# A written round for the attention loop: ordering edges on four engines, pairs and turned parts at fixed places

## The chip, the cores and the metric

The kernel runs on one core of one Trainium2 chip. The metric is device time in microseconds (us). Engines are named as the profile names them: PE (TensorE matmul), PEld (its weight load), DVE (VectorE), ACT (ScalarE), POOL (GpSimd) and SP (SyncE, which issues the DMAs). Each of them takes its instructions in the order of its own queue.

## The reference, cut to what matters

Two layers of a hybrid backbone over 1024 latent tokens and 256 context tokens, width 1024. In each layer one input projection feeds three mixers (attention, a bidirectional mLSTM, a pooling mixer); their outputs are joined, projected by `w_out`, added to the residual, normalised, and a SwiGLU follows. The change touches the attention and what is run beside it:

```python
def one_block(qi):                    # 128 query rows, 8 heads of 64, 2 key/value heads
    s = einsum('bqhgd,bkhd->bhgqk', qi, k) * d ** -0.5
    p = softmax(s, -1)
    return einsum('bhgqk,bkhd->bqhgd', p, v)
...
xl = xl + g1_l * (concatenate([att_l, ml_l, pool_l], -1) @ w_out)
```

Latent queries see 1280 keys (1024 latent, 256 context). In the first layer the context queries are computed too and see 256 keys.

## The kernel before, in words

Numbers are kept as pairs of f16 (a high part and the rest), so a product is three matmuls. The program is written with a tile library: it records instructions, and a scheduler of the library then chooses, engine by engine, the order in which they stand in the queues, by a cost model of its own and by the buffers that are free.

The attention loop of a layer works through *units*. A unit is one head and one tile of 128 query rows against 1280 keys; in the first layer there are 64 of these and 4 units of four heads against 256 keys, in the second layer 64. For a unit:

- `front` (L1303): six matmuls write the **scores** into `Sp`, three banks of PSUM with two buffers (L1311, PE). DVE takes the row maximum over 1280 columns (L1315, `mx<-Sp`) and scales it (L1320, `mx<-mx,rq`). ACT takes the **exponential** into `pf` (f32, two buffers) and adds up the rows into `sums`.
- `split` (L1330): the high part of `pf` is copied to `phl` in f16 (ACT, at L152; for one unit in eight DVE, L1339), POOL subtracts it to get the rest (`phl<-pf,phl`), and a transposing DMA on SP's queue turns `phl` into `pT` (L1345, five buffers). For ten units a layer, the *turned* ones, PE transposes `pf` in three *parts* of 4, 4 and 2 blocks into a bank `turn` (L1354), ACT copies each part to `pT` and DVE subtracts.
- `values` (L1361) takes two units, a *pair*. DVE takes the reciprocal of `sums` (L1366). PE spreads it over a bank `pv` (two matmuls, L1369, `pv<-idn,sums`) and ACT copies it out (`ao<-pv`). Then 60 matmuls (L1376) multiply `pT` by the values into another part of the same bank. DVE multiplies by the spread reciprocals (`ao<-pv,ao`), ACT copies the high part to `mixT` (`T<-ao`; mixT lies in the buffer `T1`, shown as T) and DVE subtracts for the rest (`T<-ao,T`).

One turn of the loop (L1453) writes the front of unit i, the split of unit i-1, one step of *fill*, and the values of units i-5 and i-4. A fill step (L1387) is twelve matmuls of the output projection into a bank `pwo` and one DVE addition into the residual (`X<-pwo,prm,X`). A new weight tile for it is split into its f16 parts by an ACT copy and a DVE subtraction (`hl<-st`, `hl<-st,hl`; both at helper lines L152 and L166). `budget` sets how often a step comes. Helper `bank` has two buffers, shared by `pv`, `turn`, `pwo` and the norms.

Of the kernel before, what the change touches and what calls it, by code (L numbers as in the profile page):

```python
# [9 lines left out]
F32 = mybir.dt.float32  # L10
# [8 lines left out]
P = 128  # L19
# [61 lines left out]
@with_exitstack  # L81
def hybrid_kernel(ctx: ExitStack, tc: tile.TileContext, I, out, dbg=None):
    nc = tc.nc
    V, S, G, TE, DMA = nc.vector, nc.scalar, nc.gpsimd, nc.tensor, nc.sync
    MUL, ADD, SUB, MAX, MIN = ALU.mult, ALU.add, ALU.subtract, ALU.max, ALU.min
    dbg = dbg or {}

# [33 lines left out]
    def bank3(name="S"):  # L121
        return cur["s"].tile([P, 1536], F32, tag="S", name=name)
# [10 lines left out]


    mm = TE.matmul
    order = mybir.DependencyInfo(mybir.DependencyClass.NoSync, mybir.DependencyReason.DATA)
    tabs = {"last": [], "pre": None, "kind": None}

    def after(i, j):
# [601 lines left out]
    for l in range(DEPTH):  # L741
# [555 lines left out]
        class Unit:  # L1297
# [4 lines left out]

            def front(self):  # L1303
                qt, nk, k0, n = self.qt, self.nk, self.k0, self.n
                Sp = bank3("Sp")
# [12 lines left out]
                h0 = self.hs[0]  # L1318
                if ne == 1:
                    tabs["mx"] = V.tensor_scalar(mx[:, :1], mx[:, :1], rq[:, 1, qt, h0:h0 + 1], LN4096, op0=MUL, op1=ADD).ins  # L1320
                else:
                    tt(mx[:, :ne], mx[:, :ne], rq[:, 1, qt, h0:h0 + ne], MUL)
                    tabs["mx"] = V.tensor_scalar(mx[:, :ne], mx[:, :ne], LN4096, None, op0=ADD).ins
                self.pf = pt_((P, NTOK), F32, "pf", PFB)
                for e, h in enumerate(self.hs):
                    act(self.pf[:, e * nk:(e + 1) * nk], Sp[:, e * nk:(e + 1) * nk], AF.Exp, bias=mx[:, e:e + 1],
                        scale=rq[:, 0, qt, h:h + 1],
                        accum_out=self.qs[1][:, h:h + 1])

            def split(self):  # L1330

                i, n, pf = self.i, self.n, self.pf
                if i in turned:
                    self.pT = pt_((P, 2, 10, P), F16, "pT", PTB)
                    self.parts = [self.turn(k, min(4, 10 - k)) for k in range(0, 10, 4)]
                    return
                hl = pt_((P, 2, NTOK), F16, "phl", PHB)
                if i % 8 == 0:
                    V.tensor_copy(hl[:, 0, :n], pf[:, :n])  # L1339
                else:  # L1340
                    act(hl[:, 0, :n], pf[:, :n])
                tt(hl[:, 1, :n], pf[:, :n], hl[:, 0, :n], SUB, G)
                self.pT = pt_((P, 2, 10, P), F16, "pT", PTB)
                if n == NTOK:
                    DMA.dma_start_transpose(out=self.pT.rearrange("p a k c -> p (a k) c"), in_=hl.rearrange("p a t -> p (a t)"))  # L1345
                else:
                    for a in range(2):
                        DMA.dma_start_transpose(out=self.pT[:, a, :n // P], in_=hl[:, a, :n])
# [11 lines left out]
        def values(us, pair):  # L1360

            qt, sums = us[0].qt, us[0].qs[1]
            nkt, k0 = us[0].nk // P, us[0].k0
            hs = (2 * pair, 2 * pair + 1)
            kv = pair // 2
            V.reciprocal(sums[:, hs[0]:hs[0] + 2], sums[:, hs[0]:hs[0] + 2])  # L1366
            pb = bank("pv")
            for g, h in enumerate(hs):
                mm(pb[64 * g:64 * g + 64, P:2 * P], sums[:, h:h + 1].to_broadcast([P, 64]), idn, start=True, stop=True)  # L1369
            u = f2k((P, 2, P), F32, "ao")  # L1370
            act(u[:, 0], pb[:, P:2 * P])
            for kt in range(nkt):
                for j, (a, b) in enumerate(TERMS):
                    for g, h in enumerate(hs):
                        un = us[g if len(us) == 2 else 0]
                        mm(pb[64 * g:64 * g + 64, 0:P], qkv[:, 6, b, k0 + kt * P:k0 + (kt + 1) * P][:, kv * 64:kv * 64 + 64],  # L1376
                           un.pT[:, a, un.hs.index(h) * nkt + kt], start=(kt == 0 and j == 0), stop=(kt == nkt - 1 and j == 2),
                           skip_group_check=True)
            tt(u[:, 1], pb[:, 0:P], u[:, 0], MUL)
            q = slice(qt * P, (qt + 1) * P)  # L1380
            act(mixT[:, pair, 0, q], u[:, 1])
            tt(mixT[:, pair, 1, q], u[:, 1], mixT[:, pair, 0, q], SUB)

        def wout(w, k0, m, t0, n, pb):
            for k in range(4):
# [48 lines left out]
        units = []  # L1434
# [7 lines left out]
        nt = {}  # L1442
        fill = fills()
        nu = len(units)
        turned = [u.i for u in units if len(u.hs) == 1][5::6]
        budget = 0.0
        fill_ffn = first_ffn()

# [1 line left out]

            return (1.1 if part < 0.9 else 2.5) if last else 0.8 if part < 0.2 else 1.5

        for i in range(nu + 5):  # L1453
            now[0] = i
            if i < nu:
                units[i].front()
            parts = []
            if 1 <= i <= nu:
                units[i - 1].split()
                parts = units[i - 1].parts  # L1460
            if parts:
                parts.pop(0)()
            if i >= 3:
                budget = min(budget + pace(i / nu), 3.0)
                if budget > 0:
                    c = next(fill, None)
                    if c is None:
                        c = next(fill_ffn, 0)
                    budget -= c
            if parts:  # L1470
                parts.pop(0)()
            if i >= 5:
                u = units[i - 5]
                if len(u.hs) > 1:
                    for e in range(0, len(u.hs), 2):
                        values([u], u.hs[e] // 2)
                elif u.hs[0] % 2 == 0:
                    values([u, units[i - 4]], u.hs[0] // 2)
                if u.hs[-1] in (6, 7) and u.qt < 8:
                    done[0] = u.qt  # L1480
                units[i - 5] = u = None
            while parts:
                parts.pop(0)()
            pump()
        for _ in fill:
            pass
        units = fill = None
# [544 lines left out]
```

## Time and profile before

| what | value |
|---|---|
| median of 3 runs | 2888.27 us (2887.95 to 2888.49) |
| profiled execution | 2884.12 us, its span 2882.4 us |
| PE busy over the span | 2631.7 us (91%) |
| DVE busy | 1951.8 us (68%) |
| ACT busy | 1412.3 us (49%) |
| POOL busy | 1234.7 us (43%) |
| DMA: the hardware queue | 38.4% of 16 engines |

A busy share is a mean over stages with different limits. The two attention loops lie at about 376 to 700 us and 1879 to 2170 us of the span; what bounds them is read from the timeline of those stretches, and not from the shares of the table.

### The profile page before, as it was taken

What the parts mean: (1) busy time and instruction counts of PE and PEld (TensorE: products, weight loads), DVE (VectorE), ACT (ScalarE), POOL (GpSimd) and SP (SyncE); (2) the same over time, 40 slices, a digit from 0 to 9 for tenths busy, and PEclk for the clock granted to TensorE, in tenths of its full rate; (3) what the DMA queues carried; (4) which work ended last, traced back from release to release, by engine and by line L of the source; (5) the groups of instructions that cost most, each with busy time, mean ns of one, the idle gap of its engine ahead of it and who ended that gap; (6) DMA issues with size and microseconds to landing.
All of it is one profiled execution on the core that took longest, in us unless ns stands there. A gap on an engine that the chain in (4) does not pass through costs nothing. (4 is left out here: it accounts for less than half of the span.)

```text
span 2882.4 us, 54835 instructions
## 1 busy us (share of the span) xinstructions
PE 2631.7 (91%) x21819; PEld 1521.2 (53%) x21819; DVE 1951.8 (68%) x3439; ACT 1412.3 (49%) x2816; POOL 1234.7 (43%) x959
## 2 busy tenths in 40 slices
PE   7999978887889999999999999878877799999997
PEld 4875555555545555555554674545545344444444
DVE  5458866678866565656665657877778766665666
ACT  5345556666534443434344445466666444444453
POOL 1123444455444443444443213444454554555551
PEclk9999999999999999999999999999999999999999
DMA  9534486677122222222212222487774111111211
GB/s 290 149 109 127 131 186 119 124 135 145 56 73 81 81 88 88 81 81 88 74 45 76 67 60 62 123 155 133 131 143 118 44 59 45 59 60 50 67 52 74
DMA packets 579797, 283.20 MB, mean 98 GB/s; under 512 B 311048, under 2 KB 568916, under 8 KB 579028
## 3 DMA queue, kind: packets, MB, share of 16 engines
q1 hardware_dynamic: 579364, 279.62, 38.4%
q8 instruction: 171, 2.80, 0.4%
q14 instruction: 86, 0.70, 0.1%
q10 hardware_dynamic: 176, 0.07, 0.0%
HBM read 176.19 MB, written 20.87 MB: 68 GB/s over the span
## 5 line engine op out<-in xcount | busy, mean ns | idle before, releaser
L1927 PEld LDWEIGHTS <-hlp 128*128 128x128 f16 x5040 | 492.2, 98 | 606.1 <-issue 30.5
L1927 PE MATMUL Swb<-T,hlp 128*128 128x512 f16 x1920 | 444.7, 381 | 28.7 <-DVE sg L166 13.5
L169 POOL TENSOR_TENSOR phl<-pf,phl 128x1280 f16<-128x1280 f32 (+1 forms) x112 | 292.4, 2613 | 313.7 <-ACT phl L152 209.7
L166 DVE SCALAR_TENSOR_TENSOR hlp<-ws,hlp 128x512 f16<-128x512 f32 (+1 forms) x320 | 228.4, 720 | 150.0 <-ACT hlp L152 121.8
L152 ACT ACTIVATE hlp<-ws 128x512 f16<-128x512 f32 (+1 forms) x320 | 163.6, 518 | 218.9 <-PE Swb L1927 87.6
L152 ACT ACTIVATE pf<-Sp,mx,rq 128x1280 f32<-128x1280 f32 (+1 forms) x144 | 189.9, 1320 | 129.1 <-DVE mx L1320 103.8
L1927 PE MATMUL Swc<-T,hlp 128*128 128x512 f16 x960 | 227.2, 379 | 0.0
L1927 PE MATMUL Swb<-tq,hlp 128*128 128x512 f16 x960 | 220.7, 379 | 2.3 <-ACT T L152 2.3
L1311 PE MATMUL Sp<-T 128*128 128x512 f16 (+1 forms) x800 | 182.0, 355 | 44.1 <-ACT pf L152 42.1
L1387 PE MATMUL pwo<-T,hl 128*128 128x512 f16 (+1 forms) x960 | 194.0, 350 | 30.9 <-DVE X L166 14.9
L466 PE MATMUL pfm<-T,hl 128*128 128x512 f16 (+1 forms) x1032 | 218.3, 365 | 2.6 <-ACT E L152 2.4
L1315 DVE TENSOR_REDUCE mx<-Sp 128x1 f32<-128x1280 f32 (+1 forms) x132 | 194.5, 1474 | 33.1 <-PE Sp L1311 32.5
L152 ACT ACTIVATE T<-sg 128x512 f16<-128x512 f32 (+1 forms) x170 | 100.2, 600 | 228.5 <-POOL sg L169 153.7
L166 DVE SCALAR_TENSOR_TENSOR hlp<-st,hlp 128x256 f16<-128x256 f32 (+1 forms) x201 | 141.8, 709 | 89.5 <-ACT hlp L152 74.7
L1939 PE MATMUL dx<-T,hlp 128*128 128x256 f16 x1440 | 177.9, 273 | 12.2 <-DVE hlp L166 6.4
L169 POOL TENSOR_TENSOR ws<-st 128x256 f32<-128x256 f32 (+1 forms) x97 | 102.1, 1061 | 180.4 <-DMA st<-in_w_ffn_down_dram 82.3
L169 POOL TENSOR_TENSOR X<-X,T 128x512 f32<-128x512 f32 x80 | 113.6, 1420 | 149.4 <-DVE X L166 112.2
L1927 PE MATMUL Swa<-T,hlp 128*128 128x512 f16 x720 | 169.1, 380 | 0.0
L1939 PEld LDWEIGHTS <-hlp 128*128 128x128 f16 x1440 | 139.3, 100 | 44.6 <-issue 10.8
L152 ACT ACTIVATE hlp<-st 128x256 f16<-128x256 f32 (+1 forms) x201 | 101.2, 510 | 112.8 <-PE Swb L1927 71.7
L466 PEld LDWEIGHTS <-hl 128*128 128x128 f16 x1032 | 100.8, 102 | 97.9 <-issue 21.6
L1387 PEld LDWEIGHTS <-hl 128*128 128x128 f16 x960 | 95.2, 101 | 108.4 <-issue 42.3
(327 smaller groups left out, 4969.1 us busy)
## 6 DMA issues: line engine op xcount, KB each, us to landing
T<-in_w_ada_dram SPq DMA_DIRECT2D x48, 512.0 KB
rawa<-in_w_ada_dram SPq DMA_DIRECT2D x48, 512.0 KB
st<-in_w_in_dram SPq DMA_DIRECT2D x32, 512.0 KB
st<-in_w_out_dram SPq DMA_DIRECT2D x64, 256.0 KB
st<-in_w_ffn_gate_dram SPq DMA_DIRECT2D x32, 512.0 KB
st<-in_w_ffn_up_dram SPq DMA_DIRECT2D x30, 512.0 KB
st<-in_w_ffn_down_dram SPq DMA_DIRECT2D x30, 512.0 KB
xs<-X SPq DMA_DIRECT2D x4, 2048.0 KB
```

The source lines that it names most:

```text
L152: b = S.activation(o, i, f, **kw).ins
L166: V.scalar_tensor_tensor(o, a, s, b, op0=o0, op1=o1)
L169: (e or V).tensor_tensor(o, a, b, op=op)
L466: mm(o, w[:, a, k, :], h[:, k, b, t0:t0 + n], start=(k == 0 and j == 0), stop=(k == nk - 1 and j == 2))
L1311: mm(Sp[:, e * nk + b0:e * nk + b0 + m], ql, qkv[:, 4 + h // 4, a, k0 + b0:k0 + b0 + m], start=(a == 0), stop=(a == 1), skip_group_check=True)
L1315: r = V.tensor_reduce(mx[:, :ne], Sp[:, :n].rearrange("p (e k) -> p e k", e=ne), axis=AX.X, op=MAX)
L1387: mm(pb, w[:, a, k, :], mixT[:, k0 + k, b, t0:t0 + n], start=(k == 0 and j == 0), stop=(k == 3 and j == 2))
L1927: mm(o, w[:, a, k, :], B[:, b], start=(s in "172" and k == 0 and j == 0), stop=(k == kh(i) - 1 and j == 2), skip_group_check=True)
L1939: mm(dbank[i][:, r * 256:(r + 1) * 256], w[:, a, k, :], B[:, b], start=(first and k == 0 and j == 0), stop=(not first and k == kh(i) - 1 a ...
```

## The change: what it does

Every call on DVE, ACT, POOL and PE inside the loop goes through a wrapper, and each instruction gets an ordering edge to the one before it on its engine. The scheduler can then no longer choose: each of the four queues holds the loop's instructions as they are written. DMAs have no such edges. The loop itself is written in another order, the values are split in two at a `yield`, and they are taken one turn later (units i-6 and i-5):

```diff
+            def call(*a, **k):
+                b = f(*a, **k)
+                if row["on"]:
+                    if self.key in row:
+                        tc.add_manual_dep(b.ins, row[self.key].name, order, reason="written order")
+                    row[self.key] = b.ins
+                return b
...
+    V, S, G, TE = (InRow(e, k) for k, e in enumerate((nc.vector, nc.scalar, nc.gpsimd, nc.tensor)))
...
-                if i % 8 == 0:
-                    V.tensor_copy(hl[:, 0, :n], pf[:, :n])
-                else:
-                    act(hl[:, 0, :n], pf[:, :n])
+                act(hl[:, 0, :n], pf[:, :n])
...
-            tt(u[:, 1], pb[:, 0:P], u[:, 0], MUL)
+            yield
+            o = pb[:, 2 * P:3 * P]
+            tt(o, pb[:, 0:P], u, MUL)
             q = slice(qt * P, (qt + 1) * P)
-            act(mixT[:, pair, 0, q], u[:, 1])
-            tt(mixT[:, pair, 1, q], u[:, 1], mixT[:, pair, 0, q], SUB)
+            act(mixT[:, pair, 0, q], o)
+            tt(mixT[:, pair, 1, q], o, mixT[:, pair, 0, q], SUB)
...
-        turned = [u.i for u in units if len(u.hs) == 1][5::6]
+        turned = [u.i for u in units if len(u.hs) == 1][4::6]
...
+        in_row(True)
+        parts = []
+        for i in range(nu + 6):
...
+            for g in vals:
+                next(g)
+            if 1 <= i <= nu:
+                units[i - 1].split()
+            for g in vals:
+                next(g, None)
+            if 1 <= i <= nu:
+                parts += units[i - 1].parts
+            if len(parts) > 2:
+                parts.pop(0)()
             if i < nu:
                 units[i].front()
...
             if parts:
                 parts.pop(0)()
+            if i < nu:
+                units[i].exps()
             if i >= 3:
-                budget = min(budget + pace(i / nu), 3.0)
-                if budget > 0:
+                budget = min(budget + pace(i / nu), 4.0)
+                while budget > (2.0 if vals and i < nu else 0):
```

`vals` is filled in every second turn, the *even* one of a pair of turns; the fill steps then fall into the *odd* turn, all but a few. The product `o` now lies in the PSUM bank `pv` and no longer in SBUF. A turned unit is always an even one now.

Three places show what stands in the queues. First, DVE in the second layer, around the additions of the output projection. Before:

```order
L166 SCALAR_TENSOR_TENSOR hl<-st,hl 128x512
L169 TENSOR_TENSOR ao<-pv,ao 128x128
L1315 TENSOR_REDUCE mx<-Sp 128x1
L169 TENSOR_TENSOR T_72<-ao,T_72 128x128
L1320 TENSOR_SCALAR mx<-mx,rq 128x1
L1315 TENSOR_REDUCE mx<-Sp 128x1
L1320 TENSOR_SCALAR mx<-mx,rq 128x1
L166 SCALAR_TENSOR_TENSOR X<-pwo,prm_142,X 128x512
L1315 TENSOR_REDUCE mx<-Sp 128x1
L1366 RECIPROCAL sums<-sums 128x2
```

DVE in the same layer now, from the maximum of an odd turn to that of the next even one (the wrapper's line, L96, stands for all):

```order
L96 TENSOR_REDUCE mx<-Sp 128x1
L96 TENSOR_SCALAR mx<-mx,rq 128x1
L96 SCALAR_TENSOR_TENSOR hl<-st,hl 128x512
L96 SCALAR_TENSOR_TENSOR X<-pwo,prm_142,X 128x512
L96 RECIPROCAL sums<-sums 128x2
L96 TENSOR_TENSOR pv<-pv,ao 128x128
L96 TENSOR_TENSOR T_72<-pv,T_72 128x128
L96 TENSOR_REDUCE mx<-Sp 128x1
```

The weight split and the addition into X now stand in front of the reciprocal in every pair that has them, and no maximum stands between them.

Second, ACT in the second layer's loop. Before:

```order
L152 ACTIVATE ao<-pv 128x128
L152 ACTIVATE pf,sums<-Sp,mx,rq 128x1280
L152 ACTIVATE phl<-pf 128x1280
L152 ACTIVATE T_72<-ao 128x128
L152 ACTIVATE pf,sums<-Sp,mx,rq 128x1280
L152 ACTIVATE ao<-pv 128x128
L152 ACTIVATE pf,sums<-Sp,mx,rq 128x1280
L152 ACTIVATE T_72<-ao 128x128
```

ACT in the second layer's loop now:

```order
L96 ACTIVATE pf,sums<-Sp,mx,rq 128x1280
L96 ACTIVATE phl<-pf 128x1280
L96 ACTIVATE pf,sums<-Sp,mx,rq 128x1280
L96 ACTIVATE hl<-st 128x512
L96 ACTIVATE ao<-pv 128x128
L96 ACTIVATE phl<-pf 128x1280
L96 ACTIVATE T_72<-pv 128x128
L96 ACTIVATE pf,sums<-Sp,mx,rq 128x1280
```

The copy `ao`, for which the value matmuls wait, stood between exponentials at changing distances; it now stands behind both exponentials of the pair in front.

Third, PE at a turned unit of the second layer, with buffer numbers. Before (`pf_23052` holds the exponentials of `Sp_23042`, the unit ahead of `Sp_23128`):

```order
L1311 MATMUL Sp_23128<-T2_73 128x512
L1311 LDWEIGHTS T2_73
L1311 MATMUL Sp_23128<-T2_73 128x256
L1354 MATMUL turn_23141<-idn_75,pf_23052 128x128 x4
L1387 LDWEIGHTS hl_22820
L1387 MATMUL pwo_23153<-T1_72,hl_22820 128x512
```

PE at a turned unit now (`pf_23397` holds the exponentials of `Sp_23387` itself):

```order
L96 MATMUL Sp_23387<-T2_73 128x512
L96 LDWEIGHTS T2_73
L96 MATMUL Sp_23387<-T2_73 128x256
L96 MATMUL turn_23400<-idn_75,pf_23397 128x128 x4
L96 LDWEIGHTS T2_73
L96 MATMUL Sp_23407<-T2_73 128x512
```

The first turned part stood behind the scores of the following unit; it now stands in front of them, right behind the scores of its own unit.

## Rows read from the trace of the kernel before

**Rows 1.** Busy us (instructions) per engine in the two loops, granted clock, DMA share

```profile
core 0: us, PE busy (x) PEld busy (x) DVE busy (x) ACT busy (x) POOL busy (x), PEclk, DMA share, GB/s
376.00:697.00 321.00, 268.82 (x2963) 163.59 (x2961) 229.76 (x354) 205.01 (x347) 158.53 (x70) 0.94 0.71 138
1879.00:2165.00 286.00, 234.03 (x2609) 137.63 (x2608) 213.13 (x300) 184.96 (x287) 143.25 (x59) 0.95 0.76 141
```

**Rows 2.** Maxima of each loop: duration ns min/median/max, first and last start

```profile
L1315 DVE TENSOR_REDUCE mx<-Sp x68: 1202/1481/1493, 376.0 to 697.1; 128x1 f32<-128x1280 f32 x64, 128x4 f32<-128x1024 f32 x4
...
L1315 DVE TENSOR_REDUCE mx<-Sp x64: 1469/1478/1493, 1878.8 to 2165.5; 128x1 f32<-128x1280 f32 x64
```

**Rows 3.** Timeline from 1968 us: start, us, engine, line, operation, [idle before it]

```profile
1968.21 0.20 DVE L1320 TENSOR_SCALAR mx<-mx,rq 128x1 f32<-128x1 f32 x1
...
1968.34 1.47 DVE L1315 TENSOR_REDUCE mx<-Sp 128x1 f32<-128x1280 f32 x1
1968.53 1.42 ACT L152 ACTIVATE pf<-Sp,mx,rq 128x1280 f32<-128x1280 f32 x1 [1.49 <-DVE mx L1320]
1969.85 0.21 DVE L1320 TENSOR_SCALAR mx<-mx,rq 128x1 f32<-128x1 f32 x1
...
1970.07 1.27 ACT L152 ACTIVATE phl<-pf 128x1280 f16<-128x1280 f32 x1
1970.09 1.24 PE L1311 MATMUL Sp<-T 128*128 128x512 f16 x6 [1.75 <-ACT pf L152]
...
1971.25 1.40 ACT L152 ACTIVATE pf<-Sp,mx,rq 128x1280 f32<-128x1280 f32 x1
1971.37 1.49 DVE L1315 TENSOR_REDUCE mx<-Sp 128x1 f32<-128x1280 f32 x1 [0.65 <-PE Sp L1311]
1971.47 5.34 POOL L169 TENSOR_TENSOR phl<-pf,phl 128x1280 f16<-128x1280 f32 x2 [5.53 <-ACT phl L152]
...
1972.64 0.26 ACT L152 ACTIVATE ao<-pv 128x128 f32<-128x128 f32 x1
1972.78 0.16 DVE L1366 RECIPROCAL sums<-sums 128x2 f32<-128x2 f32 x1
...
1973.10 1.86 PE L1376 MATMUL pv<-pT,T 128*64 128x128 f16 x60
...
1974.89 0.71 PE L1311 MATMUL Sp<-T 128*128 128x512 f16 x3
```

**Rows 4.** PE's waits, 370 to 2190 us: us in total, times, longest

```profile
PE pv L1376 <- ACT ao L152: 13.9, 14, 2.2
```

**Rows 5.** Timeline from 1960 us: a weight split beside POOL's subtractions

```profile
1960.61 5.34 POOL L169 TENSOR_TENSOR phl<-pf,phl 128x1280 f16<-128x1280 f32 x2 [7.02 <-ACT phl L152]
...
1960.77 0.44 PE L1369 MATMUL pv<-idn,sums 128*64 128x128 f32 x4
...
1963.09 0.64 ACT L152 ACTIVATE hl<-st 128x512 f16<-128x512 f32 x1
...
1963.76 2.74 DVE L166 SCALAR_TENSOR_TENSOR hl<-st,hl 128x512 f16<-128x512 f32 x1 [1.68 <-ACT hl L152]
```

**Rows 6.** Timeline from 1953 us: a turned unit and a fill step

```profile
1953.29 1.42 ACT L152 ACTIVATE pf<-Sp,mx,rq 128x1280 f32<-128x1280 f32 x1 [1.40 <-DVE mx L1320]
...
1954.85 1.09 PE L1354 MATMUL turn<-idn,pf 128*128 128x128 f32 x8 [0.19 <-ACT pf L152]
...
1955.78 1.25 PE L1311 MATMUL Sp<-T 128*128 128x512 f16 x6
...
1958.09 2.75 PE L1387 MATMUL pwo<-T,hl 128*128 128x512 f16 x12 [0.28 <-DVE pT L169]
```

**Rows 7.** DVE by line and form, 1890 to 2170 us: busy us, mean ns

```profile
L169 DVE TENSOR_TENSOR T<-ao,T 128x128 f16<-128x128 f32 x28 | 32.9, 1175 | 6.2 <-ACT T L152 5.9
...
L166 DVE SCALAR_TENSOR_TENSOR X<-pwo,prm,X 128x512 f32<-128x512 f32 x23 | 17.1, 742 | 8.4 <-PE pwo L1387 8.4
...
L169 DVE TENSOR_TENSOR ao<-pv,ao 128x128 f32<-128x128 f32 x28 | 7.9, 283 | 13.0 <-PE pv L1376 11.6 <-PE Sp L1311 1.4
L1339 DVE CAST phl<-pf 128x1280 f16<-128x1280 f32 x7 | 6.4, 917 | 3.7 <-ACT pf L152 3.7
```

**Rows 8.** The same groups by line, 376 to 697 us

```profile
L169 DVE TENSOR_TENSOR T<-ao,T 128x128 f16<-128x128 f32 x36 | 28.6, 799 | 8.2 <-ACT T L152 8.1
```

More of the change, by code (lines that the diff above doesn't have):

```diff
@@ L83, in hybrid_kernel, with __init__, __getattr__, in_row @@
     nc = tc.nc
-    V, S, G, TE, DMA = nc.vector, nc.scalar, nc.gpsimd, nc.tensor, nc.sync
+    order = mybir.DependencyInfo(mybir.DependencyClass.NoSync, mybir.DependencyReason.DATA)
+    row = {"on": False}
+    class InRow:
+        def __init__(self, e, key):
+            self.e, self.key = e, key
+        def __getattr__(self, name):
+            f = getattr(self.e, name)
+            def call(*a, **k):
[5 more added lines that the diff above has]
+                return b
+            return call
+    def in_row(on):
+        row.clear()
+        row["on"] = on
+    V, S, G, TE = (InRow(e, k) for k, e in enumerate((nc.vector, nc.scalar, nc.gpsimd, nc.tensor)))
+    DMA = nc.sync
     MUL, ADD, SUB, MAX, MIN = ALU.mult, ALU.add, ALU.subtract, ALU.max, ALU.min
@@ L135, in hybrid_kernel @@
     mm = TE.matmul
-    order = mybir.DependencyInfo(mybir.DependencyClass.NoSync, mybir.DependencyReason.DATA)
     tabs = {"last": [], "pre": None, "kind": None}
@@ L1304, in front @@
                 qt, nk, k0, n = self.qt, self.nk, self.k0, self.n
-                Sp = bank3("Sp")
+                Sp = self.Sp = bank3("Sp")
                 for e, h in enumerate(self.hs):
@@ L1323, in front, with exps @@
                     tabs["mx"] = V.tensor_scalar(mx[:, :ne], mx[:, :ne], LN4096, None, op0=ADD).ins
+                self.mx = mx
+            def exps(self):
+                nk, qt, mx, Sp = self.nk, self.qt, self.mx, self.Sp
                 self.pf = pt_((P, NTOK), F32, "pf", PFB)
+                self.mx = self.Sp = None
                 for e, h in enumerate(self.hs):
@@ L1369, in values @@
                 mm(pb[64 * g:64 * g + 64, P:2 * P], sums[:, h:h + 1].to_broadcast([P, 64]), idn, start=True, stop=True)
-            u = f2k((P, 2, P), F32, "ao")
-            act(u[:, 0], pb[:, P:2 * P])
+            u = f2k((P, P), F32, "ao")
+            act(u, pb[:, P:2 * P])
             for kt in range(nkt):
@@ L1451, in pace @@
             return (1.1 if part < 0.9 else 2.5) if last else 0.8 if part < 0.2 else 1.5
-        for i in range(nu + 5):
+        in_row(True)
+        parts = []
+        for i in range(nu + 6):
             now[0] = i
+            vals = []
+            if i >= 6:
+                u = units[i - 6]
+                if len(u.hs) > 1:
+                    vals = [values([u], h // 2) for h in u.hs[::2]]
+                elif u.hs[0] % 2 == 0:
+                    vals = [values([u, units[i - 5]], u.hs[0] // 2)]
+                if u.hs[-1] in (6, 7) and u.qt < 8:
+                    done[0] = u.qt
+                units[i - 6] = u = None
+            for g in vals:
[8 more added lines that the diff above has]
+                parts.pop(0)()
             if i < nu:
                 units[i].front()
[L1457 to L1460, printed above, removed]
             if parts:
                 parts.pop(0)()
+            if i < nu:
+                units[i].exps()
             if i >= 3:
-                budget = min(budget + pace(i / nu), 3.0)
-                if budget > 0:
+                budget = min(budget + pace(i / nu), 4.0)
+                while budget > (2.0 if vals and i < nu else 0):
                     c = next(fill, None)
@@ L1468, in hybrid_kernel @@
                         c = next(fill_ffn, 0)
+                    if not c:
+                        break
                     budget -= c
[L1470 to L1483, printed above, removed]
             pump()
+        in_row(False)
         for _ in fill:
```

## The prediction

> **What bounds the kernel now.** I read the two attention loops alone, since the change touches nothing else. First the busy table: in the two loops PE is busy 269 of 321 us and 234 of 286 us, DVE 230 and 213, the DMA engines 71% and 76% of the time, and the clock that PE is granted averages 0.94 and 0.95 [rows 1]. No engine is full; if PE never waited, 52 + 52 = 104 us would be gone, and that is the most a better order could bring at the same work. Second the pace: from the first maximum to the last it is 321.1 us for 67 steps and 286.7 us for 63 [rows 2], together 607.8 us for 130 units or 65 pairs: 9.35 us a pair, with turned units, weight splits and norms in it. Third the timeline, for the delay from each step to the next [rows 3]: with four queues in a fixed order the loop runs at the length of the longest circle of waits, and these delays are what such a circle is made of.
>
> **The circle in the new order.** ACT's queue in a pair is exponential of the even unit, its copy `phl`, exponential of the odd unit, then `ao` of the next values. The 60 value matmuls wait for `ao`: bank `pv` holds both, and this wait is in the trace already, 14 times [rows 4]. On PE the scores of the next even unit stand behind these matmuls, and their maximum, its scaling and the exponential follow: the circle is closed. Its length [rows 3]: exponential to copy 1.54 (1968.53 to 1970.07), copy to the next exponential 1.18, that to `ao` 1.39, `ao` to the value matmuls 0.46, these to the scores behind them 1.79, scores to maximum 1.28 (1970.09 to 1971.37), maximum to scaling 1.51, scaling to exponential 0.32. Sum 9.47 us a pair. In the kernel before, `ao` could be slipped between exponentials and the scores could run in front of the values; now nothing may pass.
>
> In such a plain pair the rest lies beside the circle. The odd unit's scores follow the even one's at once, its maximum is done before ACT is free, and fill (2.75 us, [rows 6]), addition and reciprocal fit between. DVE's two operations on the product come before the next scores end. The copies of one unit in eight go from DVE (0.917 us, [rows 7]) to ACT, where they are in the 1.18 above. `o` in PSUM: the subtraction `T<-ao,T` takes a mean of 1175 and 799 ns now [rows 7, 8], though the product of the same size takes 283 ns. I take it at about that size afterwards, and cost the gain at nothing, because DVE then waits for the scores instead.
>
> **What is added to the circle.** I counted the pairs in the new DVE queue: 66 pairs, of these 20 with a turned unit and 46 without; 23 of the 46 split a weight tile.
>
> A weight split (23 pairs). ACT's half stands behind the odd exponential, DVE's half waits for it, and the addition and the reciprocal stand behind DVE's half. From the even exponential's start: odd exponential 1.54 + 1.18 = 2.72, ACT's half 4.11 (where `ao` would have been), DVE's half 0.67 later, 4.78 [rows 5]. By then POOL is at the even unit's subtraction: it starts 1.40 behind the copy (1970.07 to 1971.47, [rows 3]), at 2.94, and takes 5.34 / 2 = 2.67 [rows 5], to 5.61. In the trace DVE's half, 2.74 us long, ended 0.55 after POOL's end (1966.50 against 1965.95), so I end it at 6.16. Addition 0.74 [rows 7], reciprocal 0.16 [rows 3], a hop of 0.04 (scores end 1971.33, maximum starts 1971.37), the spreading matmuls 0.44 [rows 5], a hop: `ao` at 7.58 and not 4.11, so 3.47 us. If POOL didn't hold it back and the half took 0.74, like the addition of the same size, it would be 2.83. The Trainium skill, page SBUF — State Buffer, section SBUF: two separate sides, says that VectorE with two SBUF inputs and GpSimd take a shared pair of ports as a lock for a whole instruction; the 2.74 us agree with it.
>
> A turned unit (20 pairs). PE now waits with the first part for the even exponential, and the odd unit's scores stand behind it. The part starts 1.56 after the exponential; eight blocks took 0.93 until the scores behind them, so four take 0.46 [rows 6]: scores at 2.02, maximum 3.30, scaling 4.81, odd exponential 5.13, `ao` 6.52 instead of 4.11. That is 2.41 us where there is no fill (4 pairs). With a fill behind the second part (2.02 + 1.24 + 0.46 + 2.75 = 6.47), addition, reciprocal, hops and spreading: `ao` at 7.93, 3.82 us (5 pairs). With a weight split too: ACT's half at 6.52, DVE's from 7.19 to 7.93 without POOL in the way, `ao` at 9.35, 5.24 us (11 pairs).
>
> Thirteen odd turns of the first layer queue a second, half-wide addition: 0.47 us each by half of the columns, rounded up, 6 us.
>
> **The sum.** 66 × 9.47 = 625.0; 23 × 3.47 = 79.8; 4 × 2.41 = 9.6; 5 × 3.82 = 19.1; 11 × 5.24 = 57.6: 791.1 us, for 65 pairs 779, with the additions 785. Before it was 607.8: +177 us. The profiled execution took 2884.12 us, so 3061; the median of the runs shown is 4.15 us above it: **3065 us**. A further turn of delay at each loop's end and PE's clock are set at zero. The bounds: if all these additions hid beside other work, 65 × 9.47 = 615.5 and +8 us; upwards the clock (below). If half of the additions hide, about 2980.
>
> **Rivals.**
> - *DVE's relief decides.* If the circle is shorter than I make it and DVE is what holds the loops, the shorter subtraction gives 28 × (1.175 - 0.283) + 36 × (0.799 - 0.283) = 43.6 us, and the copies 6.4 in the second loop [rows 7, 8]: 50 us less, 2838. For it: DVE is busy 72% to 75% there [rows 1], and those waits are real. Against it: no delay of the circle is DVE waiting for POOL, and in the new order DVE itself waits for scores and for ACT. The rule of the Trainium skill's page SBUF — State Buffer, quoted above, speaks for this rival: by it the shorter form is free of POOL everywhere, 43.6 us.
> - *The bare circle.* The additions are hidden because the following pair takes the time back: +8 us, 2896. For it: ACT and PE have idle time in a pair. Against it: every addition delays `ao`, and `ao` has no slack in a circle.
> - *The clock falls as well.* PE would be busy 503 of 785 us, 64% and not 83%, with idle stretches of over 3 us at each turned unit (scores end 1.24 after their start, the part starts 1.28 + 1.51 + 0.32 + 1.56 = 4.67 after it). If the granted clock fell from 0.945 to 0.75, the 1.79 + 1.24 = 3.03 us of matmuls in the circle would grow by 3.03 × (0.945 / 0.75 - 1) = 0.79 us in 65 pairs, 51 us: 3116. For it: in the loops the clock is below 1 already. The Trainium skill, TensorE: Matmul & The Clock Gate, Part 1, says that the clock halves when the array has been idle and comes back with work; no row here shows what it does at 64%.
>
> That the change doesn't do what it says is ruled out by the queues: they hold the instructions as written.
>
> **How the numbers follow.** Forecast 0.70, clock 0.12, bare circle 0.08, DVE's relief 0.10. A measurement of this kernel can tell about 0.2% (6 us) from no change. Slower: forecast, clock and five eighths of the bare circle, 0.87; same: the rest of it, 0.03; faster: 0.10. The range leaves out DVE's relief and most of the bare circle and takes in the case of half of the additions and the clock's: 2950 to 3130.
>
> **What would show it.** In the changed kernel's profile the maxima of each loop should stand 5.8 to 6.2 us apart in the mean instead of 4.8 and 4.6, and PE should be busy about 64% there. In plain pairs `ao` should start right behind the odd exponential; in pairs with a weight split it should come about 3.5 us later, with DVE's `hl` ending half a microsecond behind POOL; at turned units the first `turn` should follow an idle stretch of PE of about 3.4 us. The subtraction `T<-pv,T` should be near 0.3 us. If the maxima stand less than 4.7 us apart, or `ao` runs between two exponentials, the circle is wrong and with it the forecast.

## The result, and the profile after

| what | before | changed kernel |
|---|---|---|
| median | 2888.11 us (2885.46 to 2888.49, 4 runs) | 3194.41 us (3192.71 to 3195.71, 4 runs) |
| ratio | | 1.1062, 95% interval 1.1043 to 1.1082 |
| span of the profiled execution | 2882.4 us | 3190.7 us |
| the two loops, first to last maximum | 321.1 + 286.7 = 607.8 us | 458.4 + 432.5 = 890.9 us |

The kernel became slower, as forecast, but by 306 us and not by 177; the range (to 3130) does not hold the time. The loops account for 283 us, the stretches outside them for the rest.

The busy table of the two loops, to be read against [rows 1]: PE is busy 68% and 64% of the loops, where it was 84% and 82%; the clock that it is granted is 0.82 and 0.83 and not 0.94 and 0.95.

```profile
376.00:834.00 458.00, 313.19 (x3033) 201.12 (x3032) 197.46 (x349) 220.49 (x359) 159.68 (x70) 0.82 0.50 97
2032.00:2465.00 433.00, 277.27 (x2737) 176.56 (x2736) 187.45 (x305) 206.39 (x307) 150.87 (x64) 0.83 0.49 99
```

The maxima, against [rows 2]: as many and as long, but 6.84 and 6.87 us apart in the mean (458.4 / 67, 432.5 / 63), where 5.8 to 6.2 was expected.

```profile
L96 DVE TENSOR_REDUCE mx<-Sp x68: 1217/1491/1492, 375.3 to 833.7; 128x1 f32<-128x1280 f32 x64, 128x4 f32<-128x1024 f32 x4
...
L96 DVE TENSOR_REDUCE mx<-Sp x64: 1474/1491/1492, 2032.5 to 2465.0; 128x1 f32<-128x1280 f32 x64
```

A plain pair in the timeline (start, us, engine, line, operation), to be laid beside [rows 3]. It closes as the circle says: exponential 2117.32, copy 2118.86, odd exponential 2120.04, `ao` right behind it at 2121.43, values 2121.75, scores 2123.55, the next maximum 2124.84. The maximum of this pair started at 2115.47: 9.37 us, 9.47 were forecast. The 60 value matmuls take 1.87 us, as they did before.

```profile
2115.47 1.49 DVE L96 TENSOR_REDUCE mx<-Sp 128x1 f32<-128x1280 f32 x1 [0.18 <-PE Sp L96]
...
2117.32 1.42 ACT L96 ACTIVATE pf<-Sp,mx,rq 128x1280 f32<-128x1280 f32 x1 [2.36 <-DVE mx L96]
...
2118.86 1.27 ACT L96 ACTIVATE phl<-pf 128x1280 f16<-128x1280 f32 x1
...
2120.04 1.40 ACT L96 ACTIVATE pf<-Sp,mx,rq 128x1280 f32<-128x1280 f32 x1
...
2121.43 0.26 ACT L96 ACTIVATE ao<-pv 128x128 f32<-128x128 f32 x1
...
2121.75 1.87 PE L96 MATMUL pv<-pT,T 128*64 128x128 f16 x60 [1.20 <-ACT ao L96]
...
2123.55 1.25 PE L96 MATMUL Sp<-T 128*128 128x512 f16 x6
...
2124.84 1.49 DVE L96 TENSOR_REDUCE mx<-Sp 128x1 f32<-128x1280 f32 x1 [0.18 <-PE Sp L96]
```

The pair in front of it, with a weight split, against [rows 5]. DVE's half ends at 2109.32, 0.55 us behind POOL (2106.16 + 2.61); the addition, the reciprocal, the spreading matmuls and `ao` follow as forecast. Then something that was not: PE has stood for 4.96 us, and the spreading takes 0.69 and not 0.44, the same 60 value matmuls 2.98 and not 1.87. The pair takes 14.08 us; 12.94 were forecast.

```profile
2106.16 2.61 POOL L96 TENSOR_TENSOR phl<-pf,phl 128x1280 f16<-128x1280 f32 x1 [5.53 <-ACT phl L96]
...
2107.33 0.61 ACT L96 ACTIVATE hl<-st 128x512 f16<-128x512 f32 x1
2107.98 1.34 DVE L96 SCALAR_TENSOR_TENSOR hl<-st,hl 128x512 f16<-128x512 f32 x1 [2.88 <-ACT hl L96]
2109.24 0.74 DVE L96 SCALAR_TENSOR_TENSOR X<-pwo,prm,X 128x512 f32<-128x512 f32 x1
2109.90 0.15 DVE L96 RECIPROCAL sums<-sums 128x2 f32<-128x2 f32 x1
...
2110.20 0.69 PE L96 MATMUL pv<-idn,sums 128*64 128x128 f32 x4 [4.96 <-DVE sums L96]
...
2110.93 0.28 ACT L96 ACTIVATE ao<-pv 128x128 f32<-128x128 f32 x1 [2.98 <-PE pv L96]
...
2111.26 2.98 PE L96 MATMUL pv<-pT,T 128*64 128x128 f16 x60 [0.36 <-ACT ao L96]
```

A turned pair without fill, against [rows 6]: the first part follows 3.46 us of idle PE (3.4 were forecast), and then six score matmuls take 2.34 and not 1.25, and the values 3.37.

```profile
2088.38 1.42 ACT L96 ACTIVATE pf<-Sp,mx,rq 128x1280 f32<-128x1280 f32 x1 [2.36 <-DVE mx L96]
...
2089.94 1.11 PE L96 MATMUL turn<-idn,pf 128*128 128x128 f32 x4 [3.46 <-ACT pf L96]
...
2090.85 2.34 PE L96 MATMUL Sp<-T 128*128 128x512 f16 x6
...
2096.79 3.37 PE L96 MATMUL pv<-pT,T 128*64 128x128 f16 x60 [0.57 <-ACT ao L96]
```

The last two pairs of the second loop are far longer, 24.57 and 24.14 us. In the first of them (maximum at 2414.32) four weight splits and four additions of half a width stand in front of the reciprocal, where the prediction priced one of each:

```profile
2425.59 0.68 DVE L96 SCALAR_TENSOR_TENSOR hl<-st,hl 128x512 f16<-128x512 f32 x1
2426.19 0.48 DVE L96 SCALAR_TENSOR_TENSOR X<-pwo,prm,X 128x256 f32<-128x256 f32 x1
...
2434.37 0.48 DVE L96 SCALAR_TENSOR_TENSOR X<-pwo,prm,X 128x256 f32<-128x256 f32 x1 [1.28 <-PE pwo L96]
2434.78 0.15 DVE L96 RECIPROCAL sums<-sums 128x2 f32<-128x2 f32 x1
```

PE's waits from 370 to 2470 us (total, times, longest), against [rows 4], show on what it now stands: the reciprocal of `sums`, which is queued behind the split and the addition on DVE, then `ao`, then the exponential in front of a turned part.

```profile
PE pv L96 <- DVE sums L96: 158.5, 63, 6.3
...
PE turn L96 <- ACT pf L96: 68.0, 20, 4.9
...
PE pv L96 <- ACT ao L96: 45.5, 67, 3.3
```

The subtraction has the length forecast, 0.29 us against 1.175 [rows 7]; the loop as a whole is slower all the same. DVE by form, 2040 to 2470 us:

```profile
L96 DVE SCALAR_TENSOR_TENSOR hl<-st,hl 128x512 f16<-128x512 f32 x23 | 23.6, 1024 | 49.5 <-ACT hl L96 49.5
...
L96 DVE TENSOR_TENSOR T<-pv,T 128x128 f16<-128x128 f32 x29 | 8.4, 291 | 10.0 <-ACT T L96 10.0
```

### The profile page after: what moved, and what is told of

Read it like the earlier page. It is cut to its first block, busy times and chain, and to the rows that moved or that the text cites. A ratio compares the mean times of both kernels' runs of the same rounds, so it can differ in the third digit from the quotient of the medians.

```text
span 3190.7 us, 54963 instructions
## 1 busy us (share of the span) xinstructions
PE 2721.5 (85%) x21819; PEld 1591.8 (50%) x21819; DVE 1880.1 (59%) x3422; ACT 1442.2 (45%) x2833; POOL 1227.2 (38%) x959
## 5 line engine op out<-in xcount | busy, mean ns | idle before, releaser
L96 PEld LDWEIGHTS <-hlp 128*128 128x128 f16 x6768 | 660.8, 99 | 680.1 <-issue 75.0
L96 POOL TENSOR_TENSOR phl<-pf,phl 128x1280 f16<-128x1280 f32 (+1 forms) x112 | 290.5, 2593 | 560.1 <-ACT phl L96 490.1
L96 PE MATMUL Swb<-T,hlp 128*128 128x512 f16 x1920 | 447.7, 383 | 31.7 <-ACT T L96 14.9
L96 PEld LDWEIGHTS <-T 128*64 128x64 f16 (+1 forms) x7520 | 397.1, 123 | 153.5 <-issue 107.7
L96 PEld LDWEIGHTS <-hl 128*128 128x128 f16 x2424 | 243.1, 103 | 280.8 <-issue 88.9
L96 DVE SCALAR_TENSOR_TENSOR hlp<-ws,hlp 128x512 f16<-128x512 f32 (+1 forms) x320 | 232.8, 734 | 151.2 <-ACT hlp L96 119.8
L96 ACT ACTIVATE pf<-Sp,mx,rq 128x1280 f32<-128x1280 f32 (+1 forms) x144 | 189.7, 1318 | 157.8 <-DVE mx L96 148.1
L96 ACT ACTIVATE hlp<-ws 128x512 f16<-128x512 f32 (+1 forms) x320 | 163.6, 518 | 213.2 <-PE Swb L96 87.0
L96 PE MATMUL Swc<-T,hlp 128*128 128x512 f16 x960 | 227.2, 379 | 0.0
L96 PE MATMUL pfm<-T,hl 128*128 128x512 f16 (+1 forms) x1032 | 220.3, 368 | 3.2 <-ACT E L96 3.0
L96 PE MATMUL Swb<-tq,hlp 128*128 128x512 f16 x960 | 220.5, 379 | 2.8 <-ACT T L96 2.7
L96 DVE TENSOR_REDUCE mx<-Sp 128x1 f32<-128x1280 f32 (+1 forms) x132 | 195.3, 1479 | 44.4 <-PE Sp L96 44.4
L96 PE MATMUL pwo<-T,hl 128*128 128x512 f16 (+1 forms) x960 | 193.3, 356 | 32.1 <-DVE X L96 14.4
L96 PE MATMUL pv<-pT,T 128*64 128x128 f16 x3936 | 175.4, 267 | 45.6 <-ACT ao L96 45.5
L96 ACT ACTIVATE T<-sg 128x512 f16<-128x512 f32 (+1 forms) x170 | 100.3, 600 | 235.6 <-POOL sg L96 158.2
L96 PE MATMUL Sp<-T 128*128 128x512 f16 (+1 forms) x800 | 192.6, 389 | 9.5 <-ACT pf L96 7.7
L96 DVE SCALAR_TENSOR_TENSOR hlp<-st,hlp 128x256 f16<-128x256 f32 (+1 forms) x201 | 142.0, 710 | 90.3 <-ACT hlp L96 75.3
L96 PE MATMUL dx<-T,hlp 128*128 128x256 f16 x1440 | 177.3, 273 | 8.2 <-ACT hlp L96 8.2
L96 DVE TENSOR_TENSOR pv<-pv,ao 128x128 f32<-128x128 f32 x72 | 21.5, 299 | 262.4 <-PE pv L96 180.7
L96 POOL TENSOR_TENSOR ws<-st 128x256 f32<-128x256 f32 (+1 forms) x97 | 102.6, 1066 | 185.7 <-DMA st<-in_w_ffn_down_dram 71.7
L96 PE MATMUL pv<-idn,sums 128*64 128x128 f32 x288 | 38.2, 346 | 158.5 <-DVE sums L96 158.5
L96 POOL TENSOR_TENSOR X<-X,T 128x512 f32<-128x512 f32 x80 | 112.7, 1408 | 148.2 <-DVE X L96 112.4
```

The source lines that it names most:

```text
L96: b = f(*a, **k)
```

## The experiments

All are edits of the changed kernel, but for e7, which is the kernel before with one edit. Ratios are to the kernel before, timed beside them. "Loops" are first to last maximum, of the one profiled execution.

| run | edit | median us | ratio, 95% interval | loops us |
|---|---|---|---|---|
| e1 | no edges | 2900.11 | 1.0026 (1.0013 to 1.0039) | 325.4 + 295.3 |
| e2 | turned parts moved | 3182.89 | 1.1003 (1.0967 to 1.1039) | 453.9 + 425.5 |
| e3 | weight split early | 3104.99 | 1.0734 (1.0692 to 1.0776) | 410.6 + 388.2 |
| e4 | PE kept at work | 3186.74 | 1.1016 (1.0978 to 1.1055) | 473.6 + 416.7 |
| e5 | the same, fitted to the idle time | 3146.35 | 1.0886 (1.0864 to 1.0908) | 448.0 + 395.1 |
| e6 | scores and maximum ahead of the values | 2995.45 | 1.0359 (1.0342 to 1.0376) | 358.7 + 342.5 |
| e7 | kernel before, `o` in PSUM | 2863.74 | 0.9910 (0.9895 to 0.9925) | 302.7 + 292.0 |
| e8 | e6 and e3 | 2960.26 | 1.0243 (1.0228 to 1.0258) | 355.4 + 313.6 |
| e9 | PE free | 3136.28 | 1.0835 (1.0819 to 1.0851) | 424.7 + 408.2 |
| e10 | PE and DVE free | 2885.86 | 0.9973 (0.9962 to 0.9983) | 310.8 + 275.5 |
| e11 | ACT free | 3102.18 | 1.0720 (1.0704 to 1.0736) | 424.4 + 381.5 |
| e12 | DVE free | 3086.08 | 1.0691 (1.0673 to 1.0708) | 419.3 + 391.6 |

**e1: is it the edges?**

```diff
-        in_row(True)
+        in_row(False)
```

> The changed kernel without its ordering edges; everything else as changed (loop order, values split in two, o in PSUM, copies all on ACT). Theory (circle): the loss comes from nothing being allowed to pass in the queues, so with the edges gone the library's scheduler spreads the steps again and the time returns to within 1.5% of the kernel before, 2850 to 2930 us. Rival (the new emission itself, values a turn later and turned units at even places, is what costs): it stays above 3050 us.

2900.11 us, in the range of the theory. With everything else of the change left in, the loss is 0.26%: the written order is the loss, nearly all of it.

**e9, e12, e10, e11: whose order?** One edit with four conditions; key 0 is DVE, 1 ACT, 2 POOL, 3 PE.

```diff
-                if row["on"]:
+                if row["on"] and self.key != 3:            # e9: PE free
+                if row["on"] and self.key != 0:            # e12: DVE free
+                if row["on"] and self.key not in (0, 3):   # e10: both free
+                if row["on"] and self.key != 1:            # e11: ACT free
```

> The changed kernel with the ordering edges on DVE, ACT and POOL only: on PE the scheduler may choose again, and it puts the next scores ahead of the value matmuls. Theory (the circle is closed on more than one engine): DVE's queue still holds product and subtraction of the pair in front of the next maximum, and these wait for the values: values 1.87 + product 0.35 + copy 0.35 + subtraction 0.35 = 2.9 us in place of 1.79 + 1.28 = 3.07, so a plain pair gains 0.2 us, 65 pairs 10 us; the odd scores no longer stand behind the turned part, 20 pairs gain up to 2.4 us, 48 us. Expected 3090 to 3190 us. Rival (PE's order closes the circle alone): below 3000 us.

3136.28 us, in the range of the theory. The plain pairs of the second layer take 9.23 us in the mean, where the undisturbed ones of the changed kernel take 9.4 (0.2 was expected); the four turned pairs without fill and split take 12.2 in place of 14.4. The timeline of e9 shows why so little is won: PE runs the next even unit's scores at 2219.13, ahead of the values at 2222.14, but their maximum stands in DVE's queue behind product and subtraction and starts at 2225.00, 4.63 us after the scores end.

```profile
2219.13 1.24 PE L96 MATMUL Sp<-T 128*128 128x512 f16 x6 [0.42 <-ACT pf L96]
...
2221.69 0.27 ACT L96 ACTIVATE ao<-pv 128x128 f32<-128x128 f32 x1
...
2222.14 1.86 PE L96 MATMUL pv<-pT,T 128*64 128x128 f16 x60
...
2224.15 0.30 DVE L96 TENSOR_TENSOR pv<-pv,ao 128x128 f32<-128x128 f32 x1 [3.91 <-PE pv L96]
2224.48 0.28 ACT L96 ACTIVATE T<-pv 128x128 f16<-128x128 f32 x1 [1.37 <-DVE pv L96]
2224.79 0.29 DVE L96 TENSOR_TENSOR T<-pv,T 128x128 f16<-128x128 f32 x1 [0.34 <-ACT T L96]
2225.00 1.48 DVE L96 TENSOR_REDUCE mx<-Sp 128x1 f32<-128x1280 f32 x1
```

> The changed kernel with the ordering edges on ACT, POOL and PE only, DVE alone free; the scheduler then puts DVE's half of a weight split behind the reciprocal. Theory (the circle is closed on PE and on DVE, and freeing one of them leaves the other): plain pairs stay at about 9.4 us; the split pairs lose their wait for DVE's half, 14.7 us to about 11.9 (ACT's half, 0.7 us, stays in the way), 24 pairs 66 us, the turned ones with a split up to 1.4 us, 12 pairs 17 us, and some of the clock's share comes back. Expected 3060 to 3150 us. Rival (DVE's order closes the circle alone, so that e10's whole gain is DVE's): below 2950 us.

3086.08 us, in the range: split pairs 12.3 us in the mean, plain ones of the second layer 9.2. With DVE free PE's order keeps the circle closed: in the plain pair from 2026.11 to 2035.48 (9.37 us) the scores still stand behind the values, and the maximum follows the scores.

```profile
2032.39 1.86 PE L96 MATMUL pv<-pT,T 128*64 128x128 f16 x60 [2.28 <-ACT ao L96]
...
2034.18 1.25 PE L96 MATMUL Sp<-T 128*128 128x512 f16 x6
...
2035.48 1.49 DVE L96 TENSOR_REDUCE mx<-Sp 128x1 f32<-128x1280 f32 x1 [0.18 <-PE Sp L96]
```

> The changed kernel with the ordering edges on ACT and POOL only. Theory: with PE and DVE free no queue takes values ahead of the next unit's scores and maximum any more, the circle is open, and the time comes near that of no edges at all (2900 us): 2890 to 2980 us. Rival (ACT's fixed order, spread sums behind both exponentials, holds the pace by itself): above 3050 us.

2885.86 us, 4 us below the range: with both free the loss is gone, and the kernel takes 0.27% less than before. One alone gives 58 or 108 us by the medians, both together 309: the circle was closed twice, on PE (scores behind values) and on DVE (maximum behind product and subtraction). ACT's order, kept here, costs nothing that shows; with PE and DVE held, freeing ACT gave 92 us (e11, next). In the two loops of e10 PE is busy 85% and 84% and the granted clock is above that of [rows 1]:

```profile
375.00:686.00 311.00, 264.76 (x2968) 159.63 (x2968) 197.14 (x349) 211.56 (x355) 157.56 (x69) 0.96 0.75 141
1881.00:2156.00 275.00, 232.18 (x2645) 134.54 (x2644) 178.87 (x299) 193.94 (x299) 147.40 (x61) 0.98 0.78 146
```

> The changed kernel with the ordering edges on DVE, POOL and PE only. Theory: the circle through the values, the next scores and their maximum stays closed on PE and DVE; the spread sums still wait for the reciprocal, which stands behind the odd unit's maximum on DVE, so only the ACT half of a weight split can move ahead (23 pairs, up to 1.4 us each, 32 us): 3110 to 3195 us. Rival (ACT's order is what holds `ao` back): below 3000 us.

3102.18 us, 8 us below the range. ACT's half of the split moves ahead; the 24 split pairs fall from 14.7 to 11.3 us, plain ones stay (11.4 us in the mean, 10.9 in the changed kernel). The circle of the plain pairs stays closed, as expected; the gain at a split was set too low. With ACT's half moved ahead, DVE's half is clear of POOL (734 ns in the mean of 23 in the second loop, 1024 in the changed kernel), and addition and reciprocal can be over before the odd exponential ends: seven of the thirteen split pairs of the second loop take 9.3 to 9.4 us, as long as a plain pair.

**e2: turned parts.**

```diff
-            if len(parts) > 2:
-                parts.pop(0)()
             if i < nu:
                 units[i].front()
...
             if i < nu:
                 units[i].exps()
+            if len(parts) == 2:
+                parts.pop(0)()
```

> The changed kernel with the first turned part behind the next unit's scores instead of in front of them, and the second behind the odd exponential. Theory: PE no longer waits 3.46 us with the odd scores queued behind; each of 20 turned pairs loses about 1.7 us of the circle and about 2 us of half-clock time: 60 to 80 us less than the changed kernel, 3115 to 3135 us. Rival (turned units don't sit on the circle, the half clock comes from elsewhere): less than 20 us gained, above 3175.

3182.89 us: about 12 us less, a miss, and what the rival had put down (above 3175). The turned pairs did get shorter, 15.2 us in the mean after 16.4, but the plain ones grew from 10.9 to 11.5. Moved behind the scores, the part still follows 2.38 us of idle PE; the second part's copy stands behind the odd exponential on ACT, and its subtraction in front of the reciprocal on DVE, so the values start late by another way, and at the lower clock (3.41 us):

```profile
2088.19 0.69 DVE L96 TENSOR_TENSOR pT<-turn,pT 128x512 f16<-128x512 f32 x1 [1.20 <-ACT pT L96]
2088.80 0.15 DVE L96 RECIPROCAL sums<-sums 128x2 f32<-128x2 f32 x1
2089.10 0.69 PE L96 MATMUL pv<-idn,sums 128*64 128x128 f32 x4 [3.03 <-DVE sums L96]
...
2090.16 3.41 PE L96 MATMUL pv<-pT,T 128*64 128x128 f16 x60 [0.36 <-ACT ao L96]
```

**e3: the weight split ahead of the even unit's work.** ACT's half is issued in the even turn ahead of `front`, DVE's behind the even maximum; inside the loop a fill step no longer splits the next tile itself.

```diff
         act(hv[:, 0], sv, scale=SW)
+        yield
         stt(hv[:, 1], sv, SW, hv[:, 0], MUL, SUB)
...
-        if ahead and pos["split"] < len(plan) and pos["split"] <= i + 1:
+        if ahead and not row["on"] and pos["split"] < len(plan) and pos["split"] <= i + 1:
...
+            half = None
+            if vals and i < nu and pos["split"] <= pos["use"] and plan[pos["split"]][0][0] in ("woa", "wob", "woc"):
+                half = w_halves()
+                next(half)
             if i < nu:
                 units[i].front()
+            if half is not None:
+                next(half, None)
```

> The changed kernel with each weight tile split in the even turn: ACT's half in front of the even exponential, where ACT is idle, DVE's half behind the even maximum, where POOL is between its subtractions. Theory: 24 pairs without a turned unit go from about 14.3 us to 9.5 or 10, 12 turned ones lose about 2 us each: 100 to 140 us less than the changed kernel, 3050 to 3095 us. Rival (POOL's hold on the ports moves along with the split and lands in front of a maximum): at most 50 us gained, above 3145.

3104.99 us, about 89 us less and 10 us above the range. The 24 split pairs fall from 14.69 to 11.01 us in the mean, 88 us; the turned ones stay. So the split's place is dear. The 3.7 us a pair are not its price alone, though: the clock's share of a split pair goes with them (1.4 to 2 us by e5 below), and the early place has a price of its own, since most of these pairs still take 9.9 us or more and a plain one 9.4.

**e4, e5: the clock.** Matmuls that nobody reads, into a bank of their own, where PE would stand; e5 gives as many as the idle time holds.

```diff
+        def warm(n):
+            dm = bank("warm")
+            for _ in range(n):
+                mm(dm, qkv[:, 4, 0, 0:P], qkv[:, 4, 1, 0:512], start=True, stop=True)
...
+                if i in turned:
+                    warm(14)
...
+            if i < nu and pos["split"] > was:         # e4
+                warm(18)
...
+                if idle > 1.3:                        # e5: idle worked out from the fill steps of the turn
+                    warm(int(min(idle - 0.6, 4.0) / 0.22))
```

> The changed kernel with matmuls that nobody reads in two idle stretches of PE: 14 of 512 columns behind the scores of each turned unit, 18 behind the fill step where a weight tile is split. Nothing else moves. Theory (PE's clock is the part of the loss that was set at zero): granted clock in the loops from 0.82 back to above 0.92, value matmuls at 1.87 us nearly everywhere, 60 to 100 us less than the changed kernel, 3095 to 3135 us. Rival (the excess over the forecast is longer waits and not the clock): no change or slower, 3190 to 3230 us.

> Unread matmuls again, now counted so that they end before PE is wanted: 14 behind the scores of each turned unit, and behind the fill step as many as the idle stretch of that pair holds (18 in a plain pair with a weight split, fewer where more steps or a turned unit shorten it, none elsewhere). In the run before, 18 stood there in every pair with a split and were too long in the first layer and beside turned units. Theory (clock): pairs with a split at 12.6 us in both layers instead of 14.7, turned ones without a split at 13.1 to 13.3 instead of 14.4 to 15.1, granted clock above 0.93 in both loops, 50 to 80 us less than the changed kernel: 3115 to 3145 us. Rival (the clock is worth little): 3180 or more.

e4 is a miss, 3186.74 us: 18 matmuls are longer than the idle time in many pairs of the first layer, whose loop grew by 15 us, while the second shrank by 16. e5 gave 3146.35 us, 1 us above its range. Its second loop is clean: in the same order as in the changed kernel, the granted clock is 0.97 and not 0.83, and the loop 395.1 us and not 432.5.

```profile
2025.00:2420.00 395.00, 324.35 (x3134) 186.60 (x3133) 186.70 (x304) 206.41 (x307) 151.18 (x64) 0.97 0.54 108
```

In a split pair of e5 (12.6 us) the unread matmuls fill the idle stretch, and the spreading and the values have the length of [rows 3, 5] again:

```profile
2091.93 4.05 PE L96 MATMUL warm<-T 128*128 128x512 f16 x18
...
2096.97 0.44 PE L96 MATMUL pv<-idn,sums 128*64 128x128 f32 x4 [0.99 <-DVE sums L96]
...
2097.78 1.87 PE L96 MATMUL pv<-pT,T 128*64 128x128 f16 x60 [0.37 <-ACT ao L96]
```

**e6, e8: the circle opened by hand.** All edges stay; scores and maximum of the even unit are written ahead of the values, the product behind the even exponential; e8 adds the early split of e3.

```diff
             V.reciprocal(sums[:, hs[0]:hs[0] + 2], sums[:, hs[0]:hs[0] + 2])
+            yield
...
             for g in vals:
                 next(g)
+            if i < nu:
+                units[i].front()
+            for g in vals:
+                next(g)
             if 1 <= i <= nu:
                 units[i - 1].split()
-            for g in vals:
-                next(g, None)
...
             if parts:
                 parts.pop(0)()
             if i < nu:
                 units[i].exps()
+            for g in vals:
+                next(g, None)
...
```

> The changed kernel with the even unit's scores and maximum ahead of the values (the reciprocal in front of the maximum, the product behind the even exponential, turned parts behind the scores). All edges stay. Theory (the circle is exponential, copy, exponential, ao, value matmuls, scores, maximum, exponential): without the scores behind the value matmuls it opens; plain pairs fall from 9.4 to about 7.5 us, where PE is full, pairs with a weight split to about 9, and the time to 2820 to 2900 us. Rival (any written order is too stiff, whichever circle is cut): above 3050 us.

> The scores ahead of the values, and the weight split in the even turn besides (ACT's half in front of ao, DVE's half behind the even maximum). Theory: the 3.5 us of a weight split leave the path to the reciprocal too; pairs at 7.5 to 8.5 us, 2790 to 2870 us, below the run with the scores ahead alone by 20 to 50 us. Rival (POOL's hold on the ports lands in front of the product, or PE is full already): no faster than with the scores ahead alone.

2995.45 us, some 200 of the 306 us back, but 3.6% above the kernel before; with the early split 2960.26 us, 35 us less. That both edits work, and in which direction, was right; that this order would be as good as before was wrong. In e6 the reciprocal waits behind DVE's half and the addition, and exponentials wait for a buffer that POOL still reads (21.1 us in all, 18 times). What else keeps e8 2.4% above before was not taken apart.

**e7: DVE's relief by itself.** The kernel before, with the product in the bank.

```diff
-            u = f2k((P, 2, P), F32, "ao")
-            act(u[:, 0], pb[:, P:2 * P])
+            u = f2k((P, P), F32, "ao")
+            act(u, pb[:, P:2 * P])
...
-            tt(u[:, 1], pb[:, 0:P], u[:, 0], MUL)
+            o = pb[:, 2 * P:3 * P]
+            tt(o, pb[:, 0:P], u, MUL)
...
```

> The kernel before with the product o in PSUM and nothing else changed. DVE's relief: the subtraction T falls from a mean of 0.8 and 1.2 us to about 0.3, DVE is 44 us less busy in the loops, and if DVE held them the time falls to about 2845 us. Theory (no loop of the kernel before is held by DVE, whose queue is reordered around such waits): DVE's busy time falls by as much, the time by at most 12 us, 2876 to 2890.

2863.74 us, 26 us or 0.9% less: faster than before, and than every other kernel here. In the second loop (1870 to 2160 us) the subtraction takes 285 ns and not the 1175 of [rows 7]:

```profile
L169 DVE TENSOR_TENSOR pv<-pv,ao 128x128 f32<-128x128 f32 x30 | 8.7, 291 | 9.8 <-PE pv L1376 9.8
L169 DVE TENSOR_TENSOR T<-pv,T 128x128 f16<-128x128 f32 x30 | 8.6, 285 | 12.5 <-ACT T L152 12.3
```

The gain was expected at 45 us by one side and at 12 to 0 by the other; it lies between. That the shorter subtraction made it is not shown. The scheduler is free here, and DVE's queue came out in another order in both loops. From the first maximum to the last value matmul the first loop takes 329.4 us (346.8 before), and the second, where the subtraction had shrunk most, 311.7 (314.4); there DVE's half of a weight split now takes 1877 ns in the mean where it took 1664. e1 is about 34 us slower than e7 by the ratios: so much goes with the rest of the change without its edges, again in an order that the scheduler chose anew.

## Why the prediction was right in direction and wrong in size

- **The circle: right.** 9.37 us measured against 9.47, where the matmuls have their old length. e9, e12 and e10 show its place: it is closed on PE and on DVE. The prediction named only PE's side (scores behind values). The sum does not change by this, but the cure does.
- **The weight split: right at the full clock.** 12.6 to 12.7 us in most such pairs of e5's second loop against 12.94; moving it took 3.7 us a pair, the clock's share among them (e3). DVE's half did end 0.55 us behind POOL. It was 24 pairs, not 23.
- **The turned units: right at the full clock.** In e5's second loop 12.0, 13.1 and 14.7 us (most pairs of each kind), against 9.47 + 2.41 = 11.88, + 3.82 = 13.29 and + 5.24 = 14.71. It was 4, 4 and 12 pairs, not 4, 5 and 11.
- **The failed step: "A further turn of delay at each loop's end and PE's clock are set at zero".** With the prices by kind of pair the second loop's 31 pairs come to 381.2 us; they took 430.5, 49 more. In e5, with the same order and the clock back, they took 393.1. So 37 of the 49 us are the clock's. In the first loop the pairs took 456.8 us against 396.0, 61 more; the clock's part of these was not measured cleanly. The rival "the clock falls as well" named the mechanism, was given 0.12, and sized it at 51 us: it let only the circle's 3.03 us of matmuls grow, at a clock of 0.75 spread evenly. The granted clock fell by less, to 0.82, but the half speed lies just behind the idle stretches, so it hits the matmuls for which everything waits: the values took 2.98 and 3.37 us in the pairs shown, and the spreading in the split pair and the second scores in the turned one grew too.
- **The last pairs: mis-sized.** The other 12 of the 49 us are not spread over the loop. In e5 the last two pairs took 20.8 and 25.9 us, 19 more than their price, and the first pair 4.7 less. They have four fill steps each and split four and five weight tiles, all but one of them ahead of the reciprocal, as in the changed kernel; the prediction had counted one step and one tile in a pair. In the first loop the last two pairs, with two of each, lie 11 us over their price (of the 61).
- **Left out: the values of the four-head units.** The first layer's four units against 256 keys have eight value groups, not two: the page of the changed kernel counts 72 products `pv<-pv,ao`, and I counted 66 pairs. The eleven plain pairs of that layer took 11.49 us in the mean, and 11.58 in e5 with the clock up: 22 us over their price (of the 61). Three that hold extra groups lie 12.5 us over, two that hold the eight exponentials of these units 7 us. That these are the cause is read from the order of those pairs, not tested. The second additions stand in none of the eleven.
- **The loops' ends: mis-sized.** Outside the loops 2275 us became 2300, 17 us more behind the first and 9 behind the second. All of it lies between a loop's last maximum and its last value matmul, 26 and 28 us before and 42 and 37 now; from there to the next loop, and to the end, the times are the same within 1 us. This term too was set at zero; it was not tried apart.
- **Together:** 49 + 61 + 25 - 6 (priced, but in no kind of pair) = 129 us, and 306 - 177 = 129.
- **DVE's relief: no rival to the sum.** The time did not fall by it. It is not idle in the changed order either: in the plain pair shown the subtraction ran from 2124.37 to 2124.66, while POOL subtracted from 2120.26 to 2125.60, and the next maximum started at 2124.84. With both inputs in SBUF the subtractions beside POOL took 1.31 and 1.75 us in the mean of the two loops before. Held until POOL's end, this one would have delayed that maximum by about 1 us; that is an estimate from these rows, and no run tried it. In the kernel before, the shorter form goes with 26 us less (e7), about half of the 50 given, but how much of that is its own is open.
- **The bare circle: wrong.** No pair took time back: the plain pair behind the split one shown kept its 9.37 us.

## What to carry to other kernels

With every queue in a fixed order, follow the circle of waits on each engine separately: freeing PE or DVE gave 58 and 108 us, freeing both 309, so a circle can be closed twice, and one open queue proves nothing. Price the pairs at the end of a loop by what really stands in their queues, and not by the mean pair. Price the matmuls behind each new idle stretch at the lower clock, since those are the ones that the circle waits for. And look for operations that got faster inside a change that lost: with `o` in PSUM and nothing else the kernel before took 0.9% less.

## What the runs showed of the hardware

- **PE's clock, same order, two ways.** With idle stretches of 3 to 6 us in most split and turned pairs the granted clock of the second loop was 0.83 in the mean of its two levels, 2.4 and 1.2 GHz (a third of the loop at the lower by the trace's clock records); with unread matmuls in those stretches 0.97, and the loop 37 us shorter. In the split pair shown the lower level begins with the spreading at 2110.2, behind 4.96 us of idle time. The rule that the prediction cites of the Trainium skill, TensorE: Matmul & The Clock Gate, Part 1, agrees; no row of the kernel before showed it at so low a share of busy time, and I set it at zero.
- **DVE behind POOL.** With two inputs in SBUF DVE's half took 1.34 us, ending 0.55 us behind POOL's end, in the pair shown of the changed kernel and in that of e5 alike; clear of POOL it takes 0.69 (e9). The 128x128 subtraction with both inputs in SBUF took 1314 and 1751 ns in the mean of the two loops before where it ran beside POOL, and 283 and 285 where it did not. With one input in PSUM it takes 286 to 291 ns beside POOL and 283 to 291 clear of it (e7 and the changed kernel). The Trainium skill, SBUF — State Buffer, section SBUF: two separate sides, says that the port pair is locked for a whole instruction; these times agree with it.
